# A planned decoder layer: where half a projection group stands in the program, who scales early weights, and when two loads are issued

## The chip, the cores and the metric

One core of a Trainium2 chip runs the whole layer in one launch. The metric is device time in microseconds, the median of several runs. Engines: PE (TensorE matmul) with PEld (its weight loads), DVE (VectorE), ACT (ScalarE), POOL (GpSimd) and SP (SyncE, which issues nearly all DMAs and does so in program order).

## The reference

Sixteen learned meta tokens go in front of 1024 tokens of width 1024. What matters here:

```python
h = rms_norm(h_res, pre_mix_g)
q1, q2, k1, k2, v, u = split(h @ w_in)          # 4 heads; u drives the SSM
o = rms_norm(diff_attention(rope(q1, q2, k1, k2), v, lam), subln_g)
y = gelu(s5_ssm(u)); y = rms_norm(y * sigmoid(y @ w_glu + b_glu), ssm_out_g)
h_res = h_res + rms_norm(concat(o, y) @ w_out, post_mix_g)
h = rms_norm(h_res, pre_ffn_g)
f = (silu(h @ w_gate) * (h @ w_up)) @ w_down     # d_ff = 2816
return (h_res + rms_norm(f, post_ffn_g))[:, 16:]
```

## The kernel before, in words

The order of all instructions is fixed while the program is built. Each piece of work is a Python generator (a stream), and `Plan.run` asks at each step which stream could go on earliest by its own model of the engines. A stream yields `N(tiles)` or `G(engine, tiles)`, the operands that it needs next, or `W(condition)`, a condition on what has been emitted so far. **A `W` is not a wait on the chip**: it only decides behind which other instructions, in each engine's queue, the stream's next instructions will stand. Streams that are ready at the same time go in the order of the list given to `plan.run`; `ffn_open` is the last of that list. DMAs are held back and issued on SP when the plan thinks that they could run, or all at once when a pool is closed. From the moment the flag `at` is set, `keep_warm` fills gaps that the plan foresees on PE with useless matmuls (line 1497).

Every product keeps nearly fp32 precision: an operand is split in a high and a low part, and three matmuls (hi*hi, hi*lo, lo*hi) are added.

**Projection** (`proj_stream`). The columns of w_in go in eight groups: u0, u1, qk0, v0, qk1, qk2, v1, qk3. A group takes 8 blocks of 128 tokens, each in 4 steps of 6 matmuls. Blocks 0 to 3 come before 4 to 7 in the order `STEPS`; two neighbouring blocks share a PSUM bank, which `ev_stream` evicts (ACT), rotates (POOL) and stores in `qk_d` or `v_d` (SP). The last group, qk3, serves head 3 alone, the last but one in use. While the projection runs, the SSM runs beside it, and then its gate: `glu_stream` (PE tiles `yT`, `z`), `gate_stream` and `ynorm_stream` (DVE, ACT), eight tiles in a row.

**Attention** (`kv_stream`, `score_stream` and others). When `ynorm_stream` has emitted its last tile, flag `ssm` is set; `kv_stream` then opens attention's memory, sets `at`, and loads `raw` tiles of k and q. `wo_stream` waits for `ssm` and for `proj` (the end of `ev_stream`); it opens, over the projection's memory, the tiles `part` (rows of w_out are loaded there first) and `xo`, which the SSM's share of the output projection reads.

**FFN.** Seven products in place of eight (Strassen) on 2x2 blocks: per 128 columns of w_gate or w_up, operands `u..` of the weights against tiles `B11`, `B21`, `B22`, `BT1` to `BT4` of the tokens (PSUM tiles PA, PS). Five weight operands are made early (`EARLY`, `eu_stream`): raw weights are multiplied by the norm's gain `gffT`, two instructions for each tile by `scale`, on DVE or POOL, whichever `less` finds freer. These tiles are `raw00` and `raw01` ([P, 4, 256], printed as raw) and three `early` ([P, 4, 128]). Later weights (`rr`) are scaled by four ACT instructions for each tile.

**w_down** (`w_stream`, `pb_stream`, called F here). Eleven pairs p of column blocks in chunks `CS = [2, 3, 3, 3]`. For each chunk, the seven operands come in the order A11, S3, S2, S1, A12, S4, A22; for each, and for each p, one half is read back from `fu_d` (printed dA or dS `<-fu_d`) and one is made from rows of w_down (tiles rr, Ga, Gb and three more, rq). `ahead()` at the head of each operand loads further w_down rows into every place that is free. `ffn_open` opens the memory for this when the last PA/PS product is emitted (flag `A`): nine more operand slots (`sl_add`) and the three `rq` places. `gpf` (post_ffn_g on all partitions, 512 KB) is used by `out_t` only, for the final norm.

Of the kernel before, what the change touches and what calls it, by code (L numbers as in the profile page):

```python
# [11 lines left out]
AF = mybir.ActivationFunctionType  # L12
# [5 lines left out]
P = 128  # L18
# [355 lines left out]
def N(*need):  # L374
    return need, "pe"


def W(fn):
    return fn, "pe"
# [5 lines left out]
def G(eng, *need):  # L385
    return need, eng
# [6 lines left out]
def build(tc, I, out):  # L393
# [3 lines left out]
    pe, act, dve = Eng(plan, "pe", nc.tensor), Eng(plan, "act", nc.scalar), Eng(plan, "dve", nc.vector)  # L397
    pool, sp = Eng(plan, "pool", nc.gpsimd), Eng(plan, "sp", nc.sync)
# [27 lines left out]
    flag = {}  # L426
# [8 lines left out]
    def bank(tag, name):  # L435
        yield W(lambda: bank_free(tag))
        used = {k[0] for k in held}
        b = min((j for j in slots if j not in used), key=lambda j: plan.last_use(slots[j]))
        t = T_(bank_pool[b], [P, 512], F32, b, name, 1)
        slots[b] = plan.tid(t)  # L440
        held[b, plan.tid(t)] = tag
        yield N(t)
        return t
# [7 lines left out]
    def sl_add(pool_, n):  # L451
        for _ in range(n):
            sl_free.append(len(sl_pool))
            sl_pool[len(sl_pool)] = pool_
# [10 lines left out]
    def slot_free(t):  # L465
        sl_free.append(sl_of[plan.tid(t)])
# [4 lines left out]
    def open_pool(es, name, side="left"):  # L471
        p = es.enter_context(tc.tile_pool(name=name, bufs=1, side=side, reuse_waits="tile"))
        m = Mem(plan, p)
        es.callback(m.close)
        return m
# [13 lines left out]
    gffT = cp.tile([P, KC], F32, name="gffT")  # L489
# [136 lines left out]
    groups = [("u", 0), ("u", 1), ("qk", 0), ("v", 0), ("qk", 1), ("qk", 2), ("v", 1), ("qk", 3)]  # L626
# [43 lines left out]
    def proj_part(dst, w, b, k2):  # L670
        hh, hl = hT[b]
        for k in (2 * k2, 2 * k2 + 1):
            hi, lo = w[0][:, k % 2, :], w[1][:, k % 2, :]
            pe.matmul(dst, lhsT=hh[:, k, :], rhs=hi, start=(k == 0), stop=False)
            pe.matmul(dst, lhsT=hh[:, k, :], rhs=lo, start=False, stop=False)
            pe.matmul(dst, lhsT=hl[:, k, :], rhs=hi, start=False, stop=(k == KC - 1))

    def proj_meta(ws, name):
        t = (yield from bank("m", "pm"))[:, :256]
        for k in range(KC):  # L680
            if k % 4 == 0:
                yield N()
            hi, lo = ws[k // 2]
            h = hT["m"][:, k * 48:k * 48 + P]
            pe.matmul(t, lhsT=h, rhs=hi[:, k % 2, :], start=(k == 0), stop=False)
            pe.matmul(t, lhsT=h, rhs=lo[:, k % 2, :], start=False, stop=(k == KC - 1))
        return t
# [24 lines left out]
    def proj_stream():  # L712
        for gi, g in enumerate(groups):
            ws = []
            ts = {}
            for b, k2 in STEPS0 if gi == 0 else STEPS:
                bp = b // 2
                if k2 == 0:
                    yield W(lambda: b in hT)
                    if b % 2 == 0:  # L720
                        ts[bp] = yield from bank("m", "p" + g[0])
                if k2 == len(ws):
                    yield W(lambda: len(wq) > 0)
                    ws.append(wq.pop(0))
                yield N(*hT[b], *ws[k2])
                proj_part(ts[bp][:, b % 2 * 256:b % 2 * 256 + 256], ws[k2], b, k2)
                if b == 7:
                    PJ["k"] += 1
                if k2 == 3 and b % 2 == 1:
                    evq.append((g, bp, ts.pop(bp)))  # L730
                    if bp == 1:
                        yield W(lambda: "m" in hT)
                        yield N(hT["m"])
                        evq.append((g, "m", (yield from proj_meta(ws, g[0]))))
                    yield W(lambda: len(evq) < 3)
# [607 lines left out]
    at = None  # L1343
# [599 lines left out]
    def ffn_open():  # L1943
        yield W(lambda: SP["t"] == len(pairs) and "wo" in flag)
        del wp["mx"]
        a2_es.close()
        a_es.close()
        hA = open_pool(h2_es, "hA", "right")
        for n in ("11", "21", "22", "T1", "T2", "T3", "T4"):
            BM[n] = [hA.tile([P, 4, 512], F32R, name=f"B{n}{p_}") for p_ in range(2)]  # L1950
        rsv.clear()
        rsv.update("st")
        MAXB["s"] = 8
        yield W(lambda: "om" in flag)
        rsv.clear()
        pa = open_pool(pa_es, "pa")
        sl_add(pa, 6)
        wp["pa"] = pa
        raw_add([(pa, f"rr{j}") for j in range(4)])
        yield W(lambda: "A" in flag)  # L1960
        h2_es.close()
        pb = open_pool(pb_es, "pb", "right")
        wp["acc"] = {n: [pb.tile([P, 512], F32, name=f"X{n}{q}") for q in range(4)] for n in DORD}
        wp["pb"] = pb
        MAXB["m"] = MD
        sl_add(pb, NU)
        raw_add([(pb, f"rq{j}") for j in range(NRQ)])
        yield W(lambda: "E" in flag)
        raw_add([(wp["pa"], "Ga"), (wp["pa"], "Gb")])
# [5 lines left out]
    CS = [2, 3, 3, 3]  # L1975
# [6 lines left out]
    DU = [{} for _ in range(sum(CS))]  # L1982
    rfree, rof, rlast = [], {}, {}

    def raw_add(places):
        rfree.extend(places)
# [21 lines left out]
    def less(*names):  # L2008
        return min(names, key=lambda n: plan.clk[n] + (0.6 if n == "pool" else 0.0))
# [69 lines left out]
    def uput(m, n, src):  # L2079
        u = yield from slot("u" + n, KEEP if "pa" in wp else 0)  # L2080
        yield from unit(u, src)
        units[m][n] = u

    def scale(r, d):
        for k in range(0, 4, 2):
            e = less("dve", "pool")
            yield G(e, r)
            engs[e].tensor_tensor(r[:, k:k + 2], r[:, k:k + 2],
                                  gffT[:, 4 * d + k:4 * d + k + 2, None].to_broadcast([P, 2, int(r.shape[2])]), ALU.mult)

    def comb(o, a, b, op):
        e = less("dve", "pool")
        yield G(e, a, b)
        engs[e].tensor_tensor(o, a, b, op)

    def eu_stream():
        yield W(lambda: "raw0" in wp)
        rs = wp["raw0"]
        for d in range(2):
            yield from scale(rs[d], d)  # L2100
        for e_ in EARLY:
            mm, n = e_
            r = rs[n == "A12"][:, :, 0:P]
            if mm > 0:
                yield W(lambda: e_ in wp["early"])
                r = wp["early"][e_]
                yield from scale(r, n == "A12")
            yield from uput(mm, n, r)
            wp["early"].pop(e_, None)
        flag["eu"] = True  # L2110
# [240 lines left out]
    def pb_stream():  # L2351
        yield W(lambda: "acc" in wp)
        pb = wp["pb"]
        gpf = wp["gpf"] = pb.tile([P, D], F32, name="gpf")
        sp.dma_start(out=gpf, in_=I["post_ffn_g"][0].partition_broadcast(P))
        wp["jkf"] = pb.tile([P, 512], BF16, name="jkf")
        p0 = 0
        for c, n in enumerate(CS):
            ps_ = range(p0, p0 + n)
            p0 += n  # L2360
            seq = [(name, q) for name in DORD for q in range(4)]
            if c == len(CS) - 1:
                seq = seq[:16] + [(name, q) for q in range(4) for name in DORD[4:]]
            for name, q in seq:
                qs = slice(q * P, q * P + P)
                t = yield from bank("m", "dn")
                for i, p_ in enumerate(ps_):
                    yield W(lambda: len(DU[p_].get(name, ())) == 2)
                    u = DU[p_][name]
                    yield N(u[0], u[1])  # L2370
                    pe.matmul(t, lhsT=u[0][:, 0, qs], rhs=u[1][:, 0], start=(i == 0), stop=False)
                    pe.matmul(t, lhsT=u[0][:, 0, qs], rhs=u[1][:, 1], start=False, stop=False)
                    pe.matmul(t, lhsT=u[0][:, 1, qs], rhs=u[1][:, 0], start=False, stop=(i == n - 1))
                    if q == 3:
                        slot_free(u[0])
                        slot_free(u[1])
                if c == len(CS) - 1 and name in DORD[4:]:
                    fin[name, q] = t
                else:
                    xq.append((c, name, q, t))  # L2380
# [122 lines left out]
```

## Time and profile before

| | us |
|---|---|
| median of 3 runs | 1243.21 |
| lowest, highest | 1237.95, 1244.00 |
| the profiled execution's own time | 1242.78 |
| its span | 1241.0 |
| mean granted TensorE clock | 0.990 |
| PE busy | 1193.9 |
| DVE, POOL, ACT busy | 933.6, 620.4, 594.9 |

The span runs from the first to the last instruction of the profiled execution; 1.78 us lie around it. All positions below are microseconds from the span's start. A busy PE includes the filling matmuls of line 1497. Nearly every instruction is issued by one helper, so all carry line 246, and tiles are told apart by their names.

### The profile page before, as it was taken

Reading aid. Unit: us, or ns where it says so; the run is one execution under the profiler, and the core shown is the slowest. Engines: PE = TensorE matmul, PEld = TensorE weight load, DVE = VectorE, ACT = ScalarE, POOL = GpSimd, SP = SyncE. Lnnn points to the kernel's source line nnn. Section 1 sums busy time; section 2 is a strip of 40 time slices with the busy share of each in tenths; the row PEclk is TensorE's granted clock in tenths of the full one; section 3 lists DMA queues with packets and bytes.
Section 4 is the critical chain, followed back from the end, with each engine's and each line's share of the span. In section 5 each row is a group of like instructions: output and inputs, shape, how many; then the busy total and the mean of one; then the engine's idle time right before and its main releaser. Section 6 shows DMA issues by size and latency. Waiting matters only on the chain.

```text
span 1241.0 us, 19790 instructions
## 1 busy us (share of the span) xinstructions
PE 1193.9 (96%) x6994; PEld 1016.7 (82%) x6994; DVE 933.6 (75%) x1673; ACT 594.9 (48%) x1250; POOL 620.4 (50%) x653
## 2 busy tenths in 40 slices
PE   8999999999999999888999999999999999999995
PEld 6999989988888888767788888888888878888874
DVE  5778877756767978988578777786767876566998
ACT  6423433345556655664565565555655444212223
POOL 1015546423422112456466766666766675445745
PEclk9999999999999999999999999999999999999998
DMA  8254444326322013131344443444434479867564
GB/s 247 75 115 103 97 99 109 77 83 197 132 65 77 27 51 120 55 131 46 119 170 154 149 139 136 170 153 139 149 136 171 153 264 413 297 228 254 188 236 170
DMA packets 155490, 182.90 MB, mean 147 GB/s; under 512 B 72016, under 2 KB 122480, under 8 KB 155392
## 3 DMA queue, kind: packets, MB, share of 16 engines
q1 hardware_dynamic: 153056, 177.38, 43.4%
q10 hardware_dynamic: 2336, 4.26, 0.9%
q8 instruction: 55, 0.90, 0.3%
q14 instruction: 43, 0.35, 0.1%
HBM read 117.52 MB, written 61.44 MB: 144 GB/s over the span
## 4 chain that ended last, share of the span: by engine, by line
PE 74%; DVE 12%; DMA 3%; POOL 3%; ACT 3%; issue 3%; SPq 1%; DVEq 0%; ACTq 0%; POOLq 0%
PE PS L246 20%; PE PA L246 14%; PE dn L246 9%; PE pqk L246 7%; PE mix L246 5%; PE pv L246 5%; PE pu L246 3%; DVE XS L246 3%; PE s L246 2%; PE z L246 2%; DVE XA L246 2%; PE pm L246 1%; DVE part L246 1%; PE Y L246 1%; PE aT L246 1%
## 5 line engine op out<-in xcount | busy, mean ns | idle before, releaser
L246 PE MATMUL PS<-BT,uS 128*128 128x512 f32 x792 | 191.4, 395 | 0.1
L246 PEld LDWEIGHTS PS<-BT,uS 128*128 128x128 f32 x792 | 148.6, 188 | 36.3 <-DVE BT L246 0.3
L246 PE MATMUL PA<-B,uA 128*128 128x512 f32 x528 | 131.6, 396 | 1.3 <-DVE B L246 1.3
L246 PE MATMUL dn<-dS,dS 128*128 128x512 f32 x528 | 124.9, 396 | 2.7 <-DMA dS<-fu_d 2.7
L246 PEld LDWEIGHTS dn<-dS,dS 128*128 128x128 f32 x528 | 100.3, 190 | 25.6 <-DMA dS<-fu_d 3.1
L246 PEld LDWEIGHTS PA<-B,uA 128*128 128x128 f32 x528 | 98.6, 188 | 25.6 <-DVE B L246 2.1
L246 PE MATMUL dn<-dA,dA 128*128 128x512 f32 x396 | 93.2, 392 | 1.5 <-DVE dA L246 1.5
L246 PEld LDWEIGHTS dn<-dA,dA 128*128 128x128 f32 x396 | 74.4, 188 | 18.4 <-DVE dA L246 1.9
L246 ACT CAST uS<-rr 128x512 fp32r<-128x512 f32 x84 | 50.2, 618 | 76.4 <-POOL rr L246 46.7
L246 POOL TENSOR_TENSOR uA<-rr,uA 128x512 fp32r<-128x512 f32 x34 | 50.5, 1484 | 49.4 <-ACT uA L246 40.1
L246 PE MATMUL pqk<-whi,hTh 128*128 128x256 f32 x256 | 74.3, 290 | 0.0
L246 PE MATMUL pqk<-wlo,hTh 128*128 128x256 f32 x256 | 73.1, 285 | 0.0
L246 PE MATMUL pqk<-whi,hTl 128*128 128x256 f32 x256 | 73.1, 285 | 0.0
L246 ACT ACTIVATE rr<-rr,gffT 128x256 f32<-128x256 f32 x168 | 72.3, 498 | 0.6 <-DMA rr<-in_w_up 0.6
L246 POOL TENSOR_TENSOR rr<-rr,rr 128x512 f32<-128x512 f32 x39 | 57.2, 1466 | 17.3 <-DVE rr L246 6.9
L246 PE MATMUL PS<-B,uS 128*128 128x512 f32 x264 | 65.2, 395 | 0.0
L246 PE MATMUL PA<-BT,uA 128*128 128x512 f32 x264 | 65.2, 395 | 0.0
L246 DVE TENSOR_TENSOR uA<-rr,uA 128x512 fp32r<-128x512 f32 x26 | 31.0, 1194 | 41.9 <-ACT uA L246 41.9
L246 POOL TENSOR_TENSOR uS<-rr,uS 128x512 fp32r<-128x512 f32 x34 | 49.4, 1461 | 25.6 <-ACT uS L246 25.6
L246 DVE TENSOR_TENSOR uS<-rr,uS 128x512 fp32r<-128x512 f32 x50 | 56.5, 1135 | 6.4 <-ACT uS L246 4.9
L246 PEld LDWEIGHTS PS<-B,uS 128*128 128x128 f32 x264 | 49.5, 188 | 12.1
L246 PEld LDWEIGHTS PA<-BT,uA 128*128 128x128 f32 x264 | 49.5, 188 | 12.0
(476 smaller groups left out, 3305.0 us busy)
## 6 DMA issues: line engine op xcount, KB each, us to landing
fu_d<-fS SPq DMA_DIRECT2D x44, 512.0 KB, 2.8
dS<-fu_d SPq DMA_DIRECT2D x44, 512.0 KB, 5.5
fu_d<-fA SPq DMA_DIRECT2D x33, 512.0 KB, 3.0
dA<-fu_d SPq DMA_DIRECT2D x33, 512.0 KB, 5.1
rr<-in_w_up SPq DMA_DIRECT2D x22, 512.0 KB, 4.2
rr<-in_w_gate SPq DMA_DIRECT2D x20, 512.0 KB, 4.7
rr<-in_w_down SPq DMA_DIRECT2D x10, 512.0 KB, 4.9
raw<-qk_d SPq DMA_DIRECT2D x6, 768.0 KB, 6.0
```

The source lines that it names most:

```text
L246: r = real(*a, **kw)
```

## The change

In the last group, blocks 4 to 7 are emitted only after flag `at` is set. The early weight tiles are scaled by four ACT instructions each (one for each of the four 128-row slices of k) in place of two on DVE or POOL. The three `rq` places are given to `ahead()` only when both halves of operand S3 of the first chunk's last pair have been emitted, and the load of `gpf` moves from the start of `pb_stream` to its second chunk. Flag `rq` is read nowhere.

```diff
@@ proj_stream
                 if k2 == 0:
                     yield W(lambda: b in hT)
+                    if gi == len(groups) - 1 and b >= 4:
+                        yield W(lambda: "at" in flag)
                     if b % 2 == 0:
                         ts[bp] = yield from bank("m", "p" + g[0])
@@ ffn_open
         sl_add(pb, NU)
+        yield W(lambda: len(DU[CS[0] - 1].get("S3", ())) == 2)
+        flag["rq"] = True
         raw_add([(pb, f"rq{j}") for j in range(NRQ)])
@@
+    def scale_a(r, d):
+        for k in range(4):
+            yield G("act", r)
+            act.activation(r[:, k], r[:, k], AF.Copy, scale=gffT[:, 4 * d + k:4 * d + k + 1])
+
     def eu_stream():
...
-            yield from scale(rs[d], d)
+            yield from scale_a(rs[d], d)
...
-                yield from scale(r, n == "A12")
+                yield from scale_a(r, n == "A12")
@@ pb_stream
         gpf = wp["gpf"] = pb.tile([P, D], F32, name="gpf")
-        sp.dma_start(out=gpf, in_=I["post_ffn_g"][0].partition_broadcast(P))
         wp["jkf"] = pb.tile([P, 512], BF16, name="jkf")
         p0 = 0
         for c, n in enumerate(CS):
+            if c == 1:
+                sp.dma_start(out=gpf, in_=I["post_ffn_g"][0].partition_broadcast(P))
```

## Rows read from the trace of the kernel before

**Rows 1.** Windows: busy us of PE, PEld, DVE, ACT, POOL; granted clock, DMA share, GB/s.

```profile
295.00:335.00 40.00, 34.95 (x382) 31.80 (x381) 28.89 (x50) 27.52 (x58) 20.92 (x31) 0.91 0.61 211
335.00:500.00 165.00, 162.34 (x1027) 139.87 (x1027) 126.36 (x237) 98.73 (x229) 38.19 (x84) 1.00 0.21 65
...
545.00:591.40 46.40, 39.48 (x338) 32.52 (x336) 39.13 (x54) 24.09 (x45) 30.43 (x24) 1.00 0.15 54
591.40:1008.70 417.30, 417.30 (x1789) 335.70 (x1790) 312.35 (x358) 226.57 (x455) 275.05 (x188) 1.00 0.43 153
...
1020.40:1030.00 9.60, 6.88 (x24) 5.50 (x24) 7.50 (x9) 7.11 (x15) 7.33 (x5) 0.82 1.03 412
1030.00:1200.00 170.00, 170.00 (x741) 139.00 (x740) 122.48 (x157) 42.58 (x72) 93.88 (x65) 1.00 0.70 259
```

**Rows 2.** Windows of line 1497 alone: PE and PEld busy, clock, DMA.

```profile
295.00:335.00 40.00, 18.34 (x258) 17.67 (x258) 0.91 0.61 211
...
545.00:591.40 46.40, 12.39 (x173) 10.53 (x173) 1.00 0.15 54
```

**Rows 3.** Windows of tile pqk alone: PE, PEld, ACT busy, clock, DMA.

```profile
268.00:286.50 18.50, 3.43 (x24) 3.28 (x25) 0.00 (x0) 1.00 0.19 71
286.50:295.40 8.90, 8.79 (x72) 8.63 (x72) 0.84 (x2) 1.00 0.48 141
```

**Rows 4.** Timeline of PE before attention's first transposes: start, us, what.

```profile
295.47 2.63 PE L1497 MATMUL kT<-identb 128*128 128x128 bf16 x44
297.93 0.61 PE L246 MATMUL kT<-ident,raw 128*128 128x128 f32 x4
```

**Rows 5.** Chain that ended last, attention's start: start, us, what.

```profile
290.51 0.76 DVE ytok L246
...
292.60 6.84 DMA raw<-qk_d
...
306.22 9.77 DMA part<-in_w_out
```

**Rows 6.** Timeline of SP: start, us, DMAs issued.

```profile
295.61 5.33 SPq L191 DMA_DIRECT2D qk_d<-ev  x10
```

**Rows 7.** Windows of tile early alone: DVE, ACT, POOL busy, clock, DMA.

```profile
545.00:592.00 47.00, 3.19 (x4) 1.90 (x3) 5.02 (x3) 1.00 0.16 54
```

**Rows 8.** Windows of tile raw alone: PE, PEld, DVE, ACT, POOL busy.

```profile
490.00:500.00 10.00, 1.01 (x8) 0.64 (x6) 0.69 (x1) 0.62 (x1) 3.08 (x3) 1.00 0.01 3
```

**Rows 9.** Timeline of DVE, ACT and POOL at the last early tile.

```profile
552.82 1.50 DVE L246 TENSOR_TENSOR early<-early,gffT 128x256 f32<-128x256 f32 x1
...
555.29 0.62 ACT L246 CAST uA<-early 128x512 fp32r<-128x512 f32 x1 [4.35 <-DVE early L246]
...
559.36 1.66 POOL L246 TENSOR_TENSOR ms<-ms,mhalf 128x1 f32<-128x1 f32 x3
```

**Rows 10.** Timeline of ACT: eight scalings of later weights.

```profile
594.97 3.31 ACT L246 ACTIVATE rr<-rr,gffT 128x256 f32<-128x256 f32 x8 [0.57 <-DMA rr<-in_w_up]
```

**Rows 11.** Window where two early tiles are scaled (columns as in rows 1).

```profile
540.00:550.00 10.00, 9.22 (x53) 7.17 (x54) 9.79 (x18) 8.72 (x17) 2.61 (x3) 1.00 0.47 157
```

**Rows 12.** Timeline of SP at the opening of F.

```profile
1011.86 1.08 SPq L191 DMA_DIRECT2D gpf<-in_post_ffn_g  x1
1012.99 1.68 SPq L191 DMA_DIRECT2D rq<-in_w_down  x3
1014.73 1.91 SPq L191 DMA_DIRECT2D dS<-fu_d  x3
```

**Rows 13.** Timeline of PE in F's first chunk.

```profile
1023.14 12.17 PE L246 MATMUL dn<-dS,dS 128*128 128x512 f32 x45 [2.72 <-DMA dS<-fu_d]
1035.14 5.67 PE L246 MATMUL dn<-dA,dA 128*128 128x512 f32 x24
...
1046.09 13.99 PE L246 MATMUL dn<-dA,dA 128*128 128x512 f32 x60
```

**Rows 14.** DMA issued on SP at 1036.33: KB each, us to landing.

```profile
dA<-fu_d SPq DMA_DIRECT2D x1, 512.0 KB, 10.1
```

## The prediction

> **What bounds the kernel now.** I read the table of windows first, since its rows show where PE has slack at all. From 591.40 to 1008.70 PE is busy for all 417.30 of 417.30 us, and from 1030 to 1200 for 170.00 of 170.00, at full clock: in these stretches nothing but PE's own work counts, and whatever comes earlier at their head comes earlier at their end. From 335 to 500 it is busy 162.34 of 165.00. Slack lies in two stretches, 295 to 335 and 545 to 591 [rows 1]. The windows of line 1497, the filling matmuls, say how much: 18.34 us and 12.39 us of what counts there as busy is filling [rows 2]; so real work takes about 16.6 of 40 us at attention's start (34.95 - 18.34) and 27.1 of 46.4 ahead of the FFN. There other engines and DMAs set the pace, and the chain of waits says which: at attention's start the end of the SSM's gate on DVE, then the load of raw, later that of part [rows 5]. Ahead of the FFN the timeline has ACT standing 4.35 us for DVE's scaling of one early tile [rows 9]. A third hole, between the dense stretches, is the start of F, where PE waits 2.72 us for an operand [rows 13]. Each part of the change touches one of the three.
>
> **Part 1, the projection's second half.** Blocks 4 to 7 of the last group are 4 blocks x 4 steps x 6 = 96 matmuls. Of them, 24 now run among the gate's z matmuls, before 286.50, and 72 after, up to 295.1 [rows 3]. Because the condition is on emission, the change moves only those 24; the 72 stand behind the gate already. 72 take 8.5 us from 286.6 to 295.1, so 24 take 24 x 8.5 / 72 = 2.9 us. PE has no idle in the gate's stretch, so without them the last z ends at 283.7 instead of 286.6, if DVE and ACT, which make z's operands and free its banks, keep up. The gate's tail on DVE (ytok at 290.51) and the raw load at 292.60 follow and come earlier too. PE's own queue is no shorter: 283.7 + 96 matmuls = 283.7 + 11.4 = 295.1 again. But now it fills with filling matmuls 2.63 us before the first kT transpose at 297.93 [rows 4]; that transpose could then start at 295.1, 2.8 us sooner. So the gain lies between 0 and 2.9 us. What is late next: the ten stores of qk_d stand on SP from 295.61 and take 5.33 us [rows 6]; they follow the last pqk matmul, which does not move, and so do the loads of part, for which the projection's memory must be free and which are on the chain at 306.22 for 9.77 us [rows 5]. Against that, scores and transposes fill the start of this stretch and PE is dense from 335 on. I take 2.0 us, nearer the upper end, because the chain's first link (raw) moves whole and PE's slack of 18 us in the stretch can take the rest in any order.
>
> **Part 2, the early scaling.** Removed: on DVE 3.19 us in four instructions from 545 on [rows 7] and 0.69 us between 490 and 500; on POOL 3.08 us there [rows 8]; two more, for the first early tile, go as well. Added: 8 ACT instructions for the two raw tiles and 12 for the three early ones. Eight of the same form and 256 columns take 3.31 us, 0.41 each [rows 10]; the early ones have 128 columns, so 0.41 is their upper bound. That is 3.3 us near 490 and at most 5.0 us later.
> Where it pays is the last early tile. DVE scales it at 552.82 in 1.50 us, behind a long instruction for the residual; ACT stands idle for 4.35 us until then, casts, and only behind that POOL's own part of it and then its three reciprocal roots at 559.36 can go on, for which the last tokens' chain waits [rows 9]. With the scaling on ACT itself, in the time in which it stands idle now, the four instructions take at most 1.7 us. So of 4.35 us some 2.7 us are gained, and DVE is rid of 3.19 us in the same stretch. The upper bound is the whole wait, 4.35 us. For the lower one: the middle early tile is scaled between 540 and 550, where ACT is busy 8.72 of 10.00 [rows 11]; if its four instructions displace the squares of the chain there and nothing is won later, that costs 1.7 us. PE's filling of 12.39 us up to 591.40 shows that PE doesn't hold the stretch [rows 2], and behind it stands the dense FFN, so the gain arrives whole. I take 2.5 us, just under the 2.7. The 8 near 490 I set at nothing: DVE and POOL lose what ACT gains, PE is nearly dense up to 500 [rows 1] and hides either sign; without that cover it is 3.3 us of ACT.
> The Trainium skill (ScalarE: Activation LUTs, "Rules for kernel authors") says of multiplications to use VectorE, not ScalarE. By it this part would cost time; it is the third rival below. The trace shows the same kind of scaling on ACT beside a DVE that is busy 9.79 of 10.00 us [rows 11], which speaks for the move here.
>
> **Part 3, F's operands.** Queue order on SP decides: gpf at 1011.86, three rq rows, and at 1014.73 the operand of S2 for the second pair, for which PE stands 2.72 us until 1023.14 [rows 12, 13]. Behind the stop the next 45 matmuls take 12.00 us (1023.14 to 1035.14), while the 741 from 1030 to 1200 take 170.00 [rows 1], 0.229 each; so 45 should take 10.3, and the clock, 0.82 from 1020.4 to 1030, costs 1.7 us more. Stop and clock together are 4.4 us.
> The wait for S3 does nothing, I think: the load of S2's first pair is already emitted when the memory opens (w_stream works strictly in order, and the operand that is late is S2's second), so S3 is complete, and `ahead()` still puts the three rq rows before that operand. What changes is gpf: 1.13 us of SP's time (1011.86 to 1012.99) and 512 KB that no longer go ahead. At the 412 GB/s that the stretch from 1020.4 reaches [rows 1], these are 1.3 us. So the operand lands 1.1 us sooner at least; gpf shares the engines with the rq rows, and if the two were to be had in full, 2.4 us. The stop shrinks to between 0.3 and 1.6 us, and most of the clock's 1.7 us goes with it.
> What is late next: PE reaches operand A22 at 1046.09, and its second pair (0.7 us on, 1046.8) needs a load that SP issued at 1036.33 and that took 10.1 us, so it landed at 1046.4 [rows 13, 14]. Its margin is 0.4 us. Loads here queue for DMA bandwidth, so it moves forward only by gpf's share. The gain is therefore at most 2.4 + 0.4 = 2.8 us, at least 1.1. I take 2.0, the middle, as nothing shown is nearer to one end. gpf itself, now issued near 1046, delays loads of the second chunk by 1.3 us. I cost that at nothing, since PE waits for none of them from 1030 to 1200 [rows 1]; if their margin is as thin as A22's, it is 1.3 us, within the bounds above. gpf is needed by the final norm only. The dense stretch to 1200 hands the gain on.
>
> **Sum.** 2.0 + 2.5 + 2.0 = 6.5 us off the profiled execution's own 1242.78 (span 1241.0 and 1.78 around it): 1236.3 us. That execution stands 0.43 under the median of 1243.21. Of a kernel whose three runs lie 6 us apart, a change of under 0.5%, about 6.2 us, can hardly be told from none; the forecast lies just at that line.
>
> **Rivals.**
> 1. *The projection's part is hidden.* Attention's start waits for stores and part rows that don't move. For: both stand on the chain or ahead of it [rows 5, 6]. Against: raw is on the chain too, before them. 1242.8 - 4.5 = 1238.3.
> 2. *Slower: the projection's last steps fall behind attention's first work.* In the plan, attention's streams stand before proj_stream; once raw is there, they win, and the last steps wait for gaps. Part's memory is theirs, and its load is on the chain, so each us of delay of the last pqk matmul past 295.1 is one on the chain. The filling in 295 to 335 shows gaps to put them in anywhere up to 335 [rows 2]. If they end at 312, as late as 17 us, the time is 1242.8 + 17 - 4.5 = 1255. It cancels the other two parts at 4.5 us of delay (299.6) and is slower than the line at 10.7 (305.8). Against: 96 matmuls take 11.4 us from 283.7, and raw is not there sooner than some 11 us after the last z (297.93 - 286.6), so few steps can be left over.
> 3. *ScalarE is the bound, not DVE.* Part 2 costs its 1.7 us instead of gaining. 1242.8 - 4.0 + 1.7 = 1240.5. Against: ACT's 4.35 us of idle [rows 9].
> 4. *More of it pays*: each part near its upper bound, 2.9 + 4.35 + 2.8 = 10, so 1232.7.
>
> **Chances.** All three as summed 0.42 (1236.3, its own range 1233 to 1239); rival 1 0.20; rival 3 0.12; rival 4 0.14; slower, rival 2, 0.12. Faster by over 0.5% (under 1237.0): 0.28 of the first, all of rival 4 and a little of rival 1, 0.45. Slower: rival 2's delay past 10.7 us or a mixture, 0.12. Within: 0.43. The range holds all but rival 2 and the edges of the rest: 1230 to 1245, the low end being rival 4 with some spread of runs.
>
> **What would show it.** Part 1: no pqk matmul among the z; last z near 283.7; first kT near 295 with little filling ahead. If the last pqk matmul stands past 299, rival 2. Part 2: no ACT wait on early; first PS matmul near 587 where part 1 holds, that is 4.5 us sooner than 591.4. If it is not 2 us sooner relative to attention's start, rival 3. Part 3: rq rows still ahead of the late operand; the wait at S2 under 1.6 us; a short new one at A22 in the first chunk. The prediction is wrong if the planner's other orders from 300 to 590 move by more than these few us.

## The result and the profile after

The changed kernel takes 1249.76 us (median of 12 runs, 1244.65 to 1252.74); the kernel before, run beside it, 1242.91 (12 runs, 1237.95 to 1244.18). The ratio is 1.0058, 95% interval 1.0046 to 1.0070: 6.9 us slower, where 6.5 us faster was forecast. The profiled execution took 1252.74, the longest of its 12, with a span of 1251.0; so the 10.0 us between the two spans show where time went, and are some 3 us more than the medians differ.

Three positions divide the span: the first kT transpose of attention, the first PS matmul of the FFN, the first dn matmul of F. Before, they are 297.93, 591.39 and 1008.68; after, 300.66, 593.98 and 1014.75. So attention starts 2.7 us later, takes as long as before (293.3 against 293.5), the FFN takes 3.5 us more (420.77 against 417.29) and F 3.9 us more (236.25 against 232.32). Each of the three parts lies ahead of a stretch that lost.

The windows of after (columns as in [rows 1]):

```profile
295.00:335.00 40.00, 30.12 (x262) 26.79 (x262) 26.41 (x47) 25.87 (x54) 15.30 (x24) 0.83 0.62 210
...
640.00:700.00 60.00, 58.01 (x247) 46.10 (x246) 45.05 (x54) 32.76 (x67) 39.79 (x29) 1.00 0.43 151
...
940.00:1014.70 74.70, 73.76 (x316) 59.12 (x315) 52.97 (x61) 35.42 (x68) 53.30 (x37) 1.00 0.48 177
...
1030.00:1060.00 30.00, 27.83 (x115) 22.39 (x114) 18.64 (x21) 16.11 (x30) 19.49 (x15) 0.94 1.02 407
1060.00:1200.00 140.00, 140.00 (x610) 114.47 (x609) 102.06 (x129) 31.36 (x52) 76.92 (x54) 1.00 0.67 239
```

Attention's start has a lower clock than before (0.83 against 0.91 [rows 1]) and fewer matmuls (262 against 382, filling included). More telling: the FFN, where PE was busy for every microsecond, loses 2.0 us between 640 and 700 and 0.9 near its end.

**Attention's start.** SP's timeline of after, which answers to [rows 5, 6]:

```profile
272.02 18.29 SPq L191 DMA_DIRECT2D y_d<-ytok  x7
293.60 0.88 SPq L191 DMA_DIRECT2D qk_d<-ev  x2
294.54 0.46 SPq L191 DMA_DIRECT2D rm<-qk_d  x1
295.09 0.92 SPq L191 DMA_DIRECT2D raw<-qk_d  x2
296.12 6.41 SPq L191 DMA_DIRECT2D qk_d<-ev  x8
```

SP is through with the gate's y_d at 290.31 and then stands still for 3.3 us: next in its queue are two stores of the projection's blocks, whose rotation on POOL ends at 293.58. Behind them stand rm and raw, attention's first loads, which before went out ahead of all ten stores (raw at 292.17, stores from 295.61 [rows 6]). PE shows the price (rows of PE's timeline; in brackets the idle time before):

```profile
296.59 0.20 PE L246 MATMUL kmT<-ident,rm 16*128 16x16 f32 x1 [3.23 <-DMA rm<-qk_d]
296.73 4.14 PE L1499 MATMUL kT<-identb 128*128 128x128 bf16 x44
300.66 0.76 PE L246 MATMUL kT<-ident,raw 128*128 128x128 f32 x4
```

PE idles 3.23 us, and the same 44 filling matmuls then take 4.14 us instead of 2.63 [rows 4]. Windows of after and of before around them (columns as in [rows 1]):

```profile
296.70:300.90 4.20, 4.20 (x47) 4.18 (x47) 0.34 (x2) 0.34 (x2) 0.00 (x0) 0.60 0.97 338
```

```profile
295.50:298.10 2.60, 2.60 (x47) 2.60 (x47) 0.35 (x2) 1.01 (x4) 2.38 (x9) 1.00 1.06 386
```

The granted clock is 0.60 there in after and 1.00 before. The load of raw had landed by 299.6 (4.5 us after its issue at 295.09), so of the 2.7 us by which the first kT is later, about 1 is the slower filling.

**Inside the FFN.** What PE waited for between 594 and 1014 (us in total, times, longest); before, this list is empty:

```profile
PE PS L246 <- ACT uS L246: 2.3, 2, 1.4
PE PS L246 <- POOL uS L246: 0.6, 1, 0.6
PE PS L246 <- DVE BT L246: 0.5, 1, 0.5
```

The operand uS is late from ACT. ACT's timeline shows why: first the kernel before, then after, around the scaling of the next pair of weights.

```profile
626.21 0.58 ACT L246 COPY P<-PA 128x512 f32<-128x512 f32 x1
626.69 3.31 ACT L246 ACTIVATE rr<-rr,gffT 128x256 f32<-128x256 f32 x8
```

```profile
627.87 0.59 ACT L246 COPY P<-PA 128x512 f32<-128x512 f32 x1 [3.34 <-PE PA L246]
628.36 0.63 ACT L246 CAST uS<-rr 128x512 fp32r<-128x512 f32 x1
631.54 0.62 ACT L246 CAST fS<-Ga 128x512 fp32r<-128x512 f32 x1 [2.56 <-DVE Ga L246]
...
633.63 2.11 ACT L246 ACTIVATE rr<-rr,gffT 128x256 f32<-128x256 f32 x5
...
636.16 1.31 ACT L246 ACTIVATE rr<-rr,gffT 128x256 f32<-128x256 f32 x3
```

Before, the eight scalings follow the copy of P at once; after, they stand behind a cast of the evictions (fS), which itself waits 2.56 us for DVE, and are done at 637.5 instead of 630.0, of which only 2.6 us are the later start of the FFN. No instruction of this stretch is part of the change. What changed here is the order in which the plan put them.

**F.** PE's timeline of after, which answers to [rows 13]:

```profile
1029.54 10.60 PE L246 MATMUL dn<-dS,dS 128*128 128x512 f32 x45 [3.04 <-DMA dS<-fu_d]
...
1053.93 8.31 PE L246 MATMUL dn<-dA,dA 128*128 128x512 f32 x28 [2.17 <-DMA dA<-fu_d]
```

The stop at S2 did not shrink (3.04 us against 2.72). The 45 matmuls behind it take 10.60 us instead of 12.17, but a wait of 2.17 us appeared at A22, and the low clock now stands behind that:

```profile
1051.00:1062.00 11.00, 8.83 (x32) 6.79 (x31) 5.40 (x5) 5.35 (x10) 6.14 (x6) 0.84 1.02 411
```

SP's queue around S2:

```profile
1020.37 0.32 SPq L191 DMA_DIRECT2D fu_d<-fA  x1
1021.08 1.46 SPq L191 DMA_DIRECT2D rq<-in_w_down  x3
1022.58 1.41 SPq L191 DMA_DIRECT2D dS<-fu_d  x3
```

gpf is gone from it, but the rq rows still go first, and the store of the last fA ahead of them now goes out 5.6 us after F's start, before 2.8 us (1011.44, the issue just ahead of gpf in [rows 12], after 1008.68).

### The profile page after: what moved, and what is told of

Its sections match the earlier page's. It is cut to its first block, busy times and chain, and to the rows that moved or that the text cites. A ratio compares the mean times of both kernels' runs of the same rounds, so it can differ in the third digit from the quotient of the medians.

```text
span 1251.0 us, 19496 instructions
## 1 busy us (share of the span) xinstructions
PE 1191.2 (95%) x6843; PEld 1013.2 (81%) x6843; DVE 929.6 (74%) x1664; ACT 601.0 (48%) x1270; POOL 622.6 (50%) x652
## 4 chain that ended last, share of the span: by engine, by line
PE 25%; DVE 16%; POOL 14%; issue 12%; DMA 4%; ACT 4%; SPq 0%; POOLq 0%; DVEq 0%; ACTq 0%
PE dn L246 8%; PE mix L246 5%; POOL uA L246 3%; POOL rr L246 3%; DVE XS L246 3%; PE s L246 2%; PE pv L246 2%; PE PS L246 2%; POOL uS L246 2%; PE PA L246 2%; DVE XA L246 2%; DVE part L246 1%; DVE rr L246 1%; POOL Gb L246 1%; POOL fS L246 1%
## 5 line engine op out<-in xcount | busy, mean ns | idle before, releaser
L246 POOL TENSOR_TENSOR uS<-rr,uS 128x512 fp32r<-128x512 f32 x41 | 60.9, 1497 | 21.2 <-ACT uS L246 21.2
L246 POOL TENSOR_TENSOR uA<-rr,uA 128x512 fp32r<-128x512 f32 x30 | 43.6, 1452 | 52.6 <-ACT uA L246 47.9
L246 DVE TENSOR_TENSOR uS<-rr,uS 128x512 fp32r<-128x512 f32 x43 | 50.5, 1176 | 8.6 <-ACT uS L246 8.0
L246 DVE TENSOR_REDUCE nmx<-s 128x1 f32<-128x528 f32 (+8 forms) x60 | 48.0, 811 | 10.0 <-PE s L246 9.7
```

The source lines that it names most:

```text
L246: r = real(*a, **kw)
```

## The experiments

Each kernel was timed in 5 rounds beside the kernel before, which had medians of 1241.6 to 1242.3. The positions are those of one profiled execution each, which can lie some us off the kernel's median: 6.1 above it in `change_old_order`, 4.9 in `part1_only`, 3.0 in after, 3.3 below it in `best_try` and `part3_rq_after_S2`.

| kernel | first kT | first PS | FFN | F | median | ratio, 95% interval |
|---|---|---|---|---|---|---|
| before | 297.93 | 591.39 | 417.29 | 232.32 | 1242.91 | |
| after | 300.66 | 593.98 | 420.77 | 236.25 | 1249.76 | 1.0058 (1.0046, 1.0070) |
| part1_only | 303.93 | 597.43 | 416.88 | 234.89 | 1246.01 | 1.0030 (1.0017, 1.0044) |
| part1_raw_first | 296.37 | 589.95 | 415.60 | 234.35 | 1241.54 | 0.9995 (0.9983, 1.0007) |
| part2_only | 296.14 | 593.40 | 420.55 | 235.35 | 1250.31 | 1.0070 (1.0054, 1.0086) |
| part3_gpf_only | 296.99 | 589.93 | 415.60 | 231.67 | 1240.92 | 0.9993 (0.9976, 1.0009) |
| part2_old_order | 297.32 | 592.34 | 415.60 | 234.36 | 1242.01 | 0.9999 (0.9984, 1.0014) |
| part2_order_only | 296.71 | 597.54 | 422.11 | 235.05 | 1256.05 | 1.0111 (1.0092, 1.0130) |
| all_raw_first | 297.75 | 596.11 | 420.50 | 234.59 | 1250.24 | 1.0066 (1.0046, 1.0085) |
| parts13_raw_first | 296.34 | 588.84 | 415.60 | 232.66 | 1240.04 | 0.9986 (0.9973, 0.9999) |
| placebo_order | 296.92 | 591.44 | 420.57 | 235.39 | 1250.57 | 1.0075 (1.0053, 1.0096) |
| part2_early_only | 293.52 | 586.10 | 422.24 | 234.86 | 1246.79 | 1.0046 (1.0029, 1.0062) |
| part3_rq_after_S2 | 295.57 | 588.91 | 415.60 | 233.09 | 1242.75 | 1.0003 (0.9986, 1.0019) |
| best_try | 296.16 | 588.91 | 415.60 | 234.09 | 1243.74 | 1.0014 (1.0000, 1.0029) |
| part2_ffn_paired | 298.06 | 596.29 | 417.29 | 235.42 | 1248.96 | 1.0060 (1.0038, 1.0083) |
| placebo_paired | 299.99 | 590.29 | 418.00 | 232.21 | 1241.29 | 0.9997 (0.9982, 1.0013) |
| change_old_order | 307.04 | 597.41 | 415.60 | 234.59 | 1243.32 | 1.0018 (0.9997, 1.0040) |
| change_raw_first | 295.84 | 590.20 | 415.60 | 232.80 | 1241.16 | 1.0002 (0.9985, 1.0020) |

**Each part alone.** Edit of `part1_only`: only the hunk of `proj_stream`. Of `part2_only`: only `scale_a` and its two calls. Of `part3_gpf_only`: only the load of `gpf`. The condition on S3 needs no run: with it alone, the program has the same order on every engine and on SP as before.

> Part 1 alone, parts 2 and 3 undone. Theory A (the loss is made at attention's start: two stores of qk_d now stand ahead of attention's first loads in SP's queue): the first kT transpose at about 300.7 as with the whole change, the FFN 2 to 4 us later than before, 1245 to 1249 in all. Theory B (part 2 is the loss: ScalarE pays the scaling): part 1 alone is no slower than before, 1240 to 1243. Theory C (each edit gives the planner another order, and the FFN loses its density by chance of that order): attention's start may be as late as in A, but the loss stands in the stretch after 591, with PE waiting there for 2 us and more.

> Part 2 alone. Theory A: it keeps what the prediction gave it, 1.7 to 4.4 us ahead of the FFN; FFN's first matmul near 588 to 589.5, 1239 to 1241 in all. Theory B (ScalarE pays): 1244 to 1247, with the FFN's first matmul at 593 or later. Theory C: the FFN's first matmul earlier or the same, but PE no longer dense from there to the opening of F, which takes the gain back: 1242 to 1246.

> Part 3 without its condition on S3, which leaves the order of every queue as it is: the load of gpf moved to the second chunk alone. The prediction's step: the stop at S2's second pair shrinks from 2.7 to between 0.3 and 1.6 us, the clock's dip goes, a short wait appears at A22 (0 to 0.9 us): 1240 to 1241.7. Rival (the stop is set by the store of the last fA and the three rq rows, and the later loads of gpf and its followers delay A22's rows by 2 us, as in the whole change): the stop stays at 2.5 us or over, A22 waits 1.5 to 2.5 us, 1243 to 1245.

Part 1 costs 3.7 us, within theory A's range, with its first kT even later than that theory put it (303.93, in an execution 4.9 us above the median). Part 2 costs 8.0, more than any theory gave it, and gpf is within the noise: with it alone the stop at S2 is 2.11 us, where 0.3 to 1.6 was expected, the 45 matmuls behind it still take 12.12 us, and A22 does not wait. Part 2 loses 3.8 us between the first kT and the first PS, 3.3 in the FFN and 3.0 in F. The parts do not add: 3.7 + 8.0 - 1.4 is 10.3, the whole change 6.9.

**Part 1 with raw first.** As soon as attention's first loads are emitted, they are issued:

```diff
                 pend.append(load(jobs[n + len(pend)]))
+                if n == 0:
+                    plan.flush([plan.tid(x) for x in pend[-1] if x is not None])
```

> Part 1 alone, with the first two loads of attention issued at once, so that they stand ahead of all stores of the last group on SP. Theory A: rm and raw follow the last y_d store, near 290.4 instead of 294.5; the first kT transpose near 296 to 297 instead of 300.7; the time 3 to 5 us under that of part 1 alone, 1240 to 1243. Rival (attention's start is bound by the projection's last steps or by the later part rows, not by raw): kT earlier, but the first matmuls of the output projection and the FFN's start within 1 us of part 1 alone, and so its time.

SP's timeline of this kernel:

```profile
280.05 10.70 SPq L191 DMA_DIRECT2D y_d<-ytok  x5
290.80 0.42 SPq L191 DMA_DIRECT2D rm<-qk_d  x1
291.31 0.92 SPq L191 DMA_DIRECT2D raw<-qk_d  x2
294.05 5.66 SPq L191 DMA_DIRECT2D qk_d<-ev  x10
```

The stores stand behind, the first kT is at 296.37, and 4.5 us of time come back. So the place of two stores in SP's queue was part 1's loss, together with the order that the plan made after them: with the flush SP's order is that of before to the last DMA, without it three loads of the residual go out behind the last early load, the last of them at 560.4 (546.6 before). What is left of part 1 is 0.8 us to the good, not told apart from nothing.

**Part 2: its work without its order, and its order without its work.** In `part2_old_order` the plan books the old DVE or POOL instruction, and ScalarE gets the four real ones:

```diff
+        for k in range(0, 4, 2):
+            e = less("dve", "pool")
+            yield G(e, r)
+            plan.call(e, "tensor_tensor", lambda *a: on_act(k), (...), {})
```

Against before, PE's and SP's orders are the same to the last instruction, and those of ACT, DVE and POOL but for the scalings. `part2_order_only` is the mirror image: the plan books four ScalarE instructions, and DVE or POOL does the scaling.

> The 20 scalings run on ScalarE, but the plan is told that DVE or POOL did them, at their old cost: the order of all other instructions on every engine and on SP is that of before. So only ScalarE's real time is new. If the loss of part 2 alone (8.0 us) is ScalarE's load: about 1248 to 1251. If it is the other order that the plan makes from ScalarE's costs: within 3 us of before, and by the prediction's own working (ScalarE idle 4.35 us at the last early tile) up to 2.7 us faster: 1239 to 1244.

> The reverse: the plan is told that ScalarE scales, so that all orders are those of part 2 alone, but the scalings are done on DVE and POOL as before. If the order is the loss: 1247 to 1253, with the FFN no longer dense between 640 and 700 and F's stop at 5 us again. If ScalarE's load is: 1240 to 1244.

With the old orders part 2 costs nothing that can be told from 0 (1242.01 against 1242.16). With its orders alone, the loss is not only there but larger than the range expected, 13.9 us; part of that can be the scaling itself, which here loads DVE and POOL without the plan's knowing. So ScalarE's load is cleared; on part 2's own orders, scaling on ScalarE is even 5.7 us the better of the two (1250.31 against 1256.05). The Trainium skill (ScalarE: Activation LUTs, "Rules for kernel authors") advises VectorE for multiplications. No run here bears that out: there is no difference at the old orders, and ScalarE is the better at part 2's.

**An order with no work behind it.** In `placebo_order` the kernel before keeps all its work; only the plan's model is nudged, once:

```diff
         yield W(lambda: "raw0" in wp)
+        plan.clk["act"] += 1.0
         rs = wp["raw0"]
```

> No work of the kernel before is changed: only the plan's own clock for ScalarE is set 1.0 us forward, once, when the early weights come up. That gives other orders from there on, with two features that part 2's order has as well and the order of before has not: the last load of the residual stands behind the last early load on SP, and in the FFN the two loads of each w_gate pair are issued apart, with stores of fu_d between them. If these orders are the loss: 1247 to 1252, with PE waiting for uS near 645. If part 2's loss needs its own instructions: 1240 to 1244.

It costs 8.3 us. SP's timeline of it:

```profile
512.47 26.78 SPq L191 DMA_DIRECT2D xr<-in_x  x4
553.66 0.38 SPq L191 DMA_DIRECT2D early<-in_w_up  x1
554.09 0.55 SPq L191 DMA_DIRECT2D xr<-in_x  x1
...
618.18 7.00 SPq L191 DMA_DIRECT2D fu_d<-fA  x2
629.58 0.38 SPq L191 DMA_DIRECT2D rr<-in_w_gate  x1
630.98 0.87 SPq L191 DMA_DIRECT2D fu_d<-fS  x2
632.69 0.38 SPq L191 DMA_DIRECT2D rr<-in_w_gate  x1
```

Two features are shared with after and with part 2 alone: the last load of the residual (xr) goes out behind the last early load, at 554 to 555, where before the last of the five goes out at 546.55; and the two w_gate loads go out apart, with stores between, where before they go out together. The second is a sign of the late scaling shown above: the places that they load into come free one by one.

**Which feature costs what.** `part2_early_only` scales only the three early tiles on ScalarE; its plan has the split loads and not the late xr. `part2_ffn_paired` is part 2 with `plan.clk["dve"] += 2.0` at the FFN's second weight matrix, which puts paired loads back and leaves everything ahead of the FFN alone. `placebo_paired` is the first placebo with 2.0 for 1.0, whose order happens to have neither feature.

> Only the three early tiles (12 of the 20 instructions) are scaled on ScalarE; the two raw tiles as before. This order has the split loads of w_gate in the FFN, but not the displaced load of the residual. If each feature costs what its stretch showed in part 2 alone: about 3 us for the FFN and 1 to 3 for F, FFN's first matmul as in before (589 to 592): 1245 to 1248. If the split loads cost nothing: 1240 to 1244. If the displaced residual load is nothing and the split all: 1248 to 1251.

> Part 2 alone, with the plan's clock for DVE set 2.0 us forward at the FFN's second weight matrix. All orders up to the FFN and PE's whole order are those of part 2 alone; inside the FFN the other engines and SP go back to paired w_gate loads. If the FFN's order is what costs there: 415.6 to 417.3 us from the first PS to the first dn matmul instead of 420.6, F back to 231.7 to 234.4, and 1243 to 1246 in all, the rest being the stretch ahead of the FFN. If the FFN's loss comes from ScalarE's load or from what goes before: 420 us again and 1249 to 1251.

> No work of the kernel before is changed: as in the other placebo, ScalarE's clock in the plan is set forward, by 2.0 us instead of 1.0. Orders differ on all engines (more lines on PE and DVE than with 1.0 set), but all residual loads stay ahead of the last early load and the first w_gate loads stay paired. If those two features are the loss: within 3 us of before, 1240 to 1245. If any order other than the tuned one costs: 1247 to 1252.

The same window in `part2_only` and in `part2_ffn_paired`:

```profile
640.00:700.00 60.00, 58.11 (x248) 46.10 (x247) 45.36 (x54) 33.26 (x67) 39.84 (x29) 1.00 0.42 147
```

```profile
640.00:700.00 60.00, 60.00 (x259) 48.25 (x258) 46.16 (x56) 33.78 (x68) 38.99 (x28) 1.00 0.44 155
```

For the FFN the order is shown to be the cause: in the table every kernel with split loads takes 420.5 to 422.2 us there, every one with paired loads 415.6 to 418.0, and putting back the FFN's order alone gives 417.29. PE's waits inside the FFN say it more sharply: 2.6 to 3.5 us in the six kernels with split loads, 0 to 0.4 in the others but for `placebo_paired` (1.4). The lengths have a scatter of their own: before (417.29) and `part2_old_order` (415.60) have one PE order and no wait at all there. `part2_early_only` loses 4.9 us in the FFN and 2.5 in F (first kT to first PS 292.6, as before).

The total of `part2_ffn_paired` missed its expectation, though: 1249.0, where 1243 to 1246 was expected. That is 1.35 us under `part2_only`, and the intervals overlap; F, expected at 231.7 to 234.4, stayed at 235.42, and the stretch ahead of the FFN weighs more than I gave it (first kT to first PS 298.2, before 293.5).

In the eight kernels whose last xr stands behind the early load, the first PS comes 37.1 to 40.5 us after that xr, wherever attention began (44.8 us before). In `placebo_paired` it comes 38.1 us after an xr at 552.21, which stands ahead of the early load, and nothing is lost. What SP waited for ahead of the last xr says that the place in its queue is seldom the reason: first after (548 to 555), then `part2_only` (550 to 556), then `placebo_order` (540 to 553.9).

```profile
SPq L191 <- DVE part L246: 6.7, 1, 6.7
```

```profile
SPq L191 <- DMA h_d<-xr: 4.7, 1, 4.7
```

```profile
SPq L191 <- POOL uA L246: 14.3, 1, 14.3
```

In after and in `part2_only` the early load is out at 547.21 and 549.47, about as before (549.17), and SP then stands at the xr load itself, until an earlier row of the residual has been read or stored: the rows were late already. Only in `placebo_order` did xr stand behind an early load that waited (for POOL, until 553.66), and there the first PS is not later than before (591.44 against 591.39). So the late xr goes with the loss ahead of the FFN, more as its sign than as its cause; what makes the rows late was not tried by itself. `placebo_paired` shows that not just any other order costs.

**The whole change with other orders.** `all_raw_first`: the whole change and the flush. `change_old_order`: the whole change, part 2 booked at its old cost. `change_raw_first`: both. `parts13_raw_first`: the flush, part 2 undone.

> The whole change with attention's first two loads issued ahead of the last group's stores on SP. If the late raw is worth what it was in part 1 alone (4.5 us): 1244 to 1246.5, first kT transpose near 296 to 297. If part 2's order costs its 8 us whatever goes before it: 1248 to 1251.

> Parts 1 and 3 with attention's first loads issued ahead, part 2 undone: a try at a version under both. If the small gains add (0.8 for part 1 with raw first, 1.4 for gpf): 1239.5 to 1241, ratio 0.998. If each new order costs by itself, as part 2's does: 1243 and more.

> The whole change, with the plan told part 2's old costs, so that its orders are those of parts 1 and 3. If part 1's late raw is then the one loss left, and gpf gives its 1.4 us: 1244 to 1246.5, with the FFN dense again. If part 1's loss was masked in the whole change by part 2's: 1241 to 1244.

> The whole change, with the plan told part 2's old costs and attention's first two loads ahead of the stores: all work is moved as the change moves it, and the orders are nearly those of before. If only orders made the loss: 1239 to 1242, at or a little under before. If ScalarE's scaling costs once the rest is out of the way: 1243 to 1246.

In the whole change, raw first gains attention 2.9 us at its start and nothing at the end: the xr load goes out at 558.0 instead of 554.4, and the first PS follows it. Without part 2's orders the whole change stands at 1.0018, and with raw first as well at 1.0002: all its work is moved, and nothing is lost or won that can be told from 0. `parts13_raw_first` is the one version whose interval lies under 1, by 2.1 us and only just; one such among 17 kernels can be chance.

**F's rows one operand later.** Condition on S2 instead of S3, with gpf moved (`part3_rq_after_S2`), and the same with part 1 and raw first (`best_try`):

```diff
-        yield W(lambda: len(DU[CS[0] - 1].get("S3", ())) == 2)
+        yield W(lambda: len(DU[CS[0] - 1].get("S2", ())) == 2)
```

> Part 3 with the condition one operand later: the three rq places are given out when both halves of S2 of the first chunk's last pair have been emitted, instead of S3. On SP this moves one load of dS ahead of the three rq rows; nothing else moves on any engine against gpf alone. If the rq rows in front are what delays the operand: the stop at S2's second pair falls from about 2 to 5 us to under 1, 1238 to 1240. If the store of the last fA in front of all of them sets it: no change against gpf alone, 1240 to 1242.

> Part 1 with attention's first loads ahead of the stores, gpf moved, and rq after S2; the early tiles scaled as before. If the gains add: 1237 to 1239. If the rq condition moves a wait to A22: 1239 to 1241, as without it.

PE's timeline of `part3_rq_after_S2`:

```profile
1010.00 16.55 PE L246 MATMUL dn<-dS,dS 128*128 128x512 f32 x72
...
1037.98 0.94 PE L246 MATMUL dn<-dA,dA 128*128 128x512 f32 x3 [0.48 <-DVE Ga L246]
1041.75 8.53 PE L246 MATMUL dn<-dA,dA 128*128 128x512 f32 x29 [2.83 <-DMA dA<-fu_d]
```

The stop at S2 is gone, the 72 matmuls run through, and A22 waits 2.83 us. The rq rows were what stood in the way, and the time did not change: the stall moved to the next operand. Both totals missed what was expected: 1242.75, and 1243.74 for `best_try` (1.0014), where the gains do not add.

## Why the prediction was wrong

**The step that failed** is one that carried no number of its own: that the orders which the plan makes stay as they are beside each edit. It stands at the end of the prediction as what would make it wrong ("if the planner's other orders from 300 to 590 move by more than these few us"), at no price and with no end of the range for it; and the FFN was taken as a stretch that only hands a gain on. Orders moved from the first edit on, and past 590 as well: part 2 costs 8.0 us with its orders and 0 without them, a nudge that moves no work costs 8.3, and 3.3 us of part 2's loss stand in the very stretch that was dense.

**Part 1, -2.0 predicted, +3.7 measured alone.** PE's side came as described: all 96 pqk matmuls behind the last z, which ends 3 us sooner counted from the same store ahead of it (qk_d from rmeta, 272.67 before, 270.73 after). But the gate's tail gained only 1.3 us (ytok at 289.21 against 290.51), less than the 1.9 by which that store was early, so nothing of it is the change's: the condition "if DVE and ACT keep up" did not hold. (24 x 8.5 / 72 is 2.8, not 2.9, which changes nothing.) The 44 filling matmuls that were to give way stayed in the program: in `part1_raw_first` they run from 293.90, and the first kT follows at 296.37. And the raw load did not follow the gate. I placed all ten stores behind it because they stood there before [rows 6], and did not ask whether SP's order would stay. The second rival had the place right (attention's start) and the mechanism wrong: not late pqk matmuls, but early stores.

**Part 2, -2.5 predicted, 0 measured at equal orders.** The wait at the last early tile did go, as ACT's timeline of `part2_old_order` shows:

```profile
552.42 1.28 ACT L2099 ACTIVATE early<-early,gffT 128x128 f32<-128x128 f32 x4
553.74 0.62 ACT L246 CAST uA<-early 128x512 fp32r<-128x512 f32 x1
...
558.56 1.06 ACT L246 ACTIVATE jk<-xr 128x1024 bf16<-128x1024 f32 x1 [1.68 <-DVE xr L246]
```

The cast stands at 553.74 instead of 555.29 [rows 9]: 1.5 us, not 2.7. The four scalings took 1.28 us, less than the 1.7 allowed; but they begin only at 552.42, because the load of this tile, issued at 549.21, takes 3.1 us to land, and because the scaling of the tile before now stands on ACT ahead of them. So part of the 4.35 us was never a wait for DVE's scaling: before, the load landed 2.8 us after 549.17. Behind the cast ACT waits for DVE's residual again, and the first PS does not come sooner (592.34 against 591.39). The wait was on the chain that ended last, but a second chain, the residual over DVE and POOL, was as late: the step on DVE where the two meet starts at 559.72, before at 559.43. The third rival (ScalarE is the bound) is refuted by the same run. (The scaling on ACT that the prediction names with [rows 11] stands in [rows 10]; the former give busy times alone.)

**Part 3, -2.0 predicted, -1.4 measured for gpf alone, not told apart from 0.** Right: that the S3 condition changes nothing, that the rq rows stay in front, that A22 is next in the whole change. Wrong: that the stop at S2 is set by the queue ahead of it alone. It also depends on when the store of the last fA ahead of the rq rows goes out, which the orders decide: 5.1 to 6.1 us after F's start in the kernels with split loads, 1.9 to 4.8 in the others. Where that time is nearly the same, gpf does what the sum gave it. PE's rows of `part1_raw_first` (gpf in place, fA at 4.57 us) and of `change_raw_first` (gpf moved, 4.40):

```profile
1022.08 12.15 PE L246 MATMUL dn<-dS,dS 128*128 128x512 f32 x45 [4.81 <-DMA dS<-fu_d]
```

```profile
1020.16 10.60 PE L246 MATMUL dn<-dS,dS 128*128 128x512 f32 x45 [2.63 <-DMA dS<-fu_d]
```

The stop is 2.2 us shorter, within the 1.1 to 2.4 of the sum, and F 1.55 us (234.35 to 232.80), as A22 waits 1.41 us in the second; two executions are too few to call it shown. Mis-sized: A22's margin, 0.4 by the sum, where the whole change waits 2.17 us; and the clock's 1.7 us, which did not go but stayed (12.12 us with gpf alone) or moved behind A22's wait (0.84 in after).

The bigger F of after (3.9 us) is made of its waits: 3.04 and 2.17 us at S2 and A22, against 2.72 at S2 alone, and 1.2 us more from the last dn matmul to the end (14.8 against 13.6). In `part2_only` the stop at S2 alone is 5.35 us, 2.6 of the 3.0. What stays open is which part of the FFN's order puts off the fA store (`part2_ffn_paired`, with paired loads and fA at 3.29 us, still stops for 4.68), and what makes the residual's rows late ahead of the FFN.

## What to carry to other kernels

Where a planner or scheduler lays out the program, an edit is two changes: the work that it moves, and the order of everything that comes after. Before predicting, ask for the new order or put a price on a new one; afterwards, separate the two by booking the old cost for the new work, and measure a nudge of the plan that moves no work. And when a piece of work is put later in one engine's queue, look at each in-order queue that its results pass (here SP): what was behind may now stand in front.

## What the runs showed that was not expected

- A shift of 1.0 us in a cost model, with the same work, made the kernel 8.3 us slower (1.0075), and one of 2.0 us did nothing (0.9997).
- One profile prices no edit of 1 or 2 us here. Ten programs that are the same up to attention's start have their first kT anywhere from 293.5 to 300.0, and with the same SP order throughout the stop at S2 was 2.72 us in one kernel (before) and 4.81 in another (`part1_raw_first`).
- A late load cost more than its wait: after an idle of 3.23 us on PE, 44 filling matmuls ran at a granted clock of 0.60 and took 4.14 us instead of 2.63, and the first kT stood behind them although its operand had landed about 1 us before.
